# Sliding-window attention by key-value group, with both query blocks in one step

## The chip, the cores and the metric

The kernel runs on one core of a Trainium2 chip. The metric is the time of one execution on the device, in microseconds (us). The core has a matrix engine (PE in the profile, with its weight loads as PEld), three engines for elementwise work (DVE, ACT, POOL) and queues for transfers (DMA) between the device memory and the on-chip memory. PE writes into eight banks of accumulator memory; a bank holds 512 float32 values in each of 128 partitions, and DVE and ACT read the results from there. The granted PE clock of the profiled execution was 0.999 of full speed.

## The reference, cut to what matters

The program is one decoder layer over 256 tokens with 2048 features: a feed-forward block, a mixer (windowed attention beside a recurrent part), a look-up into a memory, a second feed-forward block and a norm. The change touches only the windowed attention inside the mixer. It has 16 query heads of 64 values, in four groups that share one key-value head each, and works in blocks of 128 queries, so there are two query blocks. A query sees at most the 128 latest positions, and each head has a learned "sink" that joins the softmax:

```python
s = jnp.einsum('bnqhgd,bnkhd->bnhgqk', qb, kb).astype(jnp.float32) * (HEAD_DIM ** -0.5)
valid = (dist >= 0) & (dist < WINDOW) & (blk * BLOCK + ki - BLOCK >= 0)
s = jnp.where(valid[None, :, None, None], s, NEG_INF)
m = jnp.maximum(jnp.max(s, axis=-1, keepdims=True), sink)
e = jnp.exp(s - m)
p = e / (jnp.sum(e, axis=-1, keepdims=True) + jnp.exp(sink - m))
o = jnp.einsum('bnhgqk,bnkhd->bnqhgd', p.astype(v.dtype), vb)
```

The first query block has 128 keys to look at, the second 256. The result, 256 tokens by 1024 values, goes into the product with `w_proj_attn`.

## The kernel before, in words

All large products go through `product` (line 420). It takes the weights two chunks of 128 rows at a time (an "item", line 401): a transfer brings the float32 chunk, ACT rounds it to a short part `hi` (line 365), DVE subtracts to get the rest `lo` (line 366), and `multiply` (line 446) issues six matmuls for each half of the tokens: `hi` by `hi` (line 442), `lo` by `hi` (line 443) and `hi` by `lo` (line 444), each 512 columns wide, or 288 in the product called "small". `AHEAD` is 2: `next_item` also writes the splitting of the next two items, and the split tiles have three buffers.

Everything else is written between those matmuls. `Interleave` (line 56) holds named groups of Python generators. After each call of `multiply` comes one `tick`, in which the first generators of each group, up to the group's limit, advance by one `yield`. The group "attn" has the limit 2, so two attention generators are under way at a time. A tick is thus six matmuls of a product and then a few steps of side work.

That is only the order of writing. The framework's planner then lays out each engine's list: at each point of its own reckoned time, an engine gets the instruction that was written first among those whose inputs and buffers the planner takes to be ready. On the chip each engine runs its list in order and waits where something is late. So side work written early can stand late in an engine's list, between the matmuls of a later tick.

The side work in question is `attend(kv, qb)` (line 940), called for four key-value groups `kv` and two query blocks `qb`, eight generators in all. Since two run at a time, the two query blocks of one group advance side by side, in the same ticks. One generator does this:

- **Scores**, line 949: the four query heads of a group are two chunks `c` by two halves `e` of the 128 partitions. Each matmul uses the 64 partitions of its half. The half `e=0` writes one bank and the half `e=1` another, both from the ring `mm`, which has three banks. The profile shows each of these float32 matmuls as two instructions.
- **Scale and mask**, line 955 (DVE), out of the banks into a tile `s`.
- **Softmax**: the maximum on DVE (line 962), small operations on four values per partition (lines 965 to 969), then the exponentials with their sums on ACT (lines 972 and 974), one for each head, and the division on DVE (lines 979 to 982).
- **Transposes**, line 988, of the probabilities through a bank of the ring `tr`, which has two banks, and a copy out on ACT (line 991).
- **Values**, line 996: 64 output partitions for each half `e`, into one `tr` bank, then a rounded copy on ACT (line 1003) and the rest on DVE (line 1004) into `ya`.

The ring `tr` also serves `feat` (line 623, the transposes at line 630) for other side work. The flag "attn", set when the last values are written, lets `decay_and_rate` (line 1055) begin, whose matmuls at line 1073 take banks from `mm`. The products under way meanwhile are "small" (288 columns, 16 ticks) and the two that make the recurrent keys (512 columns, 16 ticks each). `ya` is first needed four products later.

Of the kernel before, what the change touches and what calls it, by code (L numbers as in the profile page):

```python
# [15 lines left out]
P = 128  # L16
T = 256
# [119 lines left out]
def decoder_layer(ctx: ExitStack, tc: tile.TileContext, a: dict, out: bass.AP):  # L137
    nc = tc.nc
    act, dve, pool, pe = nc.scalar, nc.vector, nc.gpsimd, nc.tensor
# [17 lines left out]
    def f32(x):  # L157
        return x.bitcast(F32)
# [4 lines left out]
    def mm():  # L163
        return ps.tile([P, 512], F32, tag="mm", name="mm")

    def tr():
        return ps.tile([P, 512], F32, tag="tr", name="tr", bufs=2)

    def wait_for(name):
        while name not in bg.seen:  # L170
            yield

    def idle(n):
        for _ in range(n):
            yield
# [19 lines left out]
    ident = cpool.tile([P, P], F32, name="ident")  # L195
# [74 lines left out]
    for entry in weight_plan(a):  # L270
# [4 lines left out]
        w, k0, nk, c0, n = entry  # L275
# [16 lines left out]
    at = {"item": 0, "product": 0, "pool": None}  # L292
# [580 lines left out]
    with tc.tile_pool(name="mx", bufs=1, reuse_waits="tile") as sp:  # L873
# [3 lines left out]
        def t4(name, shape=(P, 4, T), dt=F32):  # L877
            return sp.tile(list(shape), dt, tag="t4", name=name, bufs=N4)
# [38 lines left out]
        qt = []  # L917
# [5 lines left out]
        kd = t4("kd")  # L923
        vt = t4("vt", (P, 2, KV_W))
# [12 lines left out]
        ya = act_tiles("ya", 2)  # L937
        sink4 = sinks[:].rearrange("p (k c e) -> p k e c", k=4, c=2)

        def attend(kv, qb):  # L940
            yield from wait_for("kv")
            w = P * (qb + 1)
            tq = slice(qb * P, qb * P + P)
            s = t4("s", (P, 2, 2, T))
            b = [mm() for _ in range(2)]
            for c in range(2):
                for e in range(2):
                    r = slice(64 * e, 64 * e + 64)
                    pe.matmul(  # L949
                        b[e][:, c * w : (c + 1) * w], qt[kv // 2][r, 2 * (kv % 2) + c, tq],  # L950
                        kd[r, kv, :w], start=True, stop=True,
                    )
            bias = abias[:, 1 - qb :, :].rearrange("p a b -> p (a b)")
            for e in range(2):
                dve.scalar_tensor_tensor(
                    s[:, e, :, :w], b[e][:, : 2 * w].rearrange("p (c w) -> p c w", c=2), 0.125,
                    bias.unsqueeze(1).to_broadcast([P, 2, w]), ALU.mult, ALU.add,
                )
            yield
            s3 = s[:].rearrange("p e c w -> p (e c) w")  # L960
            m = stat.tile([P, 4], F32, tag="m", name="m")
            dve.tensor_reduce(m[:], s3[:, :, :w], AX.X, ALU.max)
            sk = sink4[:, kv]
            m22 = m[:].rearrange("p (e c) -> p e c", e=2)
            dve.tensor_tensor(m22, m22, sk, ALU.max)
            nm = stat.tile([P, 4], F32, tag="nm", name="nm")
            dve.tensor_scalar(nm[:], m[:], -1.0, None, ALU.mult)
            es = stat.tile([P, 4], F32, tag="es", name="es")
            dve.tensor_tensor(es[:].rearrange("p (e c) -> p e c", e=2), sk, m22, ALU.subtract)
            yield  # L970
            den = stat.tile([P, 4], F32, tag="den", name="den")
            act.activation(es[:], es[:], AF.Exp)
            for i in range(4):
                at["exp"] = act.activation(
                    s3[:, i, :w], s3[:, i, :w], AF.Exp, bias=nm[:, i : i + 1],
                    accum_out=den[:, i : i + 1],
                )
            yield
            dve.tensor_tensor(den[:], den[:], es[:], ALU.add)
            dve.reciprocal(den[:], den[:])  # L980
            for i in range(4):
                dve.tensor_scalar(s3[:, i, :w], s3[:, i, :w], den[:, i : i + 1], None, ALU.mult)
            yield from idle(2)
            pt = t4("pt", (P, 2, 4, P))
            for kb in range(qb + 1):
                b = tr()
                for i in range(4):
                    pe.transpose(
                        b[:, i * P : (i + 1) * P], s3[:, i, kb * P : (kb + 1) * P], ident[:]
                    )  # L990
                act.copy(pt[:, kb], b[:].rearrange("p (i q) -> p i q", i=4))
            yield from idle(2)
            b = tr()
            for kb in range(qb + 1):
                for e in range(2):
                    pe.matmul(
                        b[64 * e : 64 * e + 64, : 2 * P], vt[:, kb, kv * 64 : kv * 64 + 64],
                        pt[:, kb, 2 * e : 2 * e + 2, :].rearrange("p c q -> p (c q)"),
                        start=kb == 0, stop=kb == qb,
                    )  # L1000
            b3 = b[:, : 2 * P].rearrange("p (c q) -> p c q", c=2)
            hi, lo = (ya.at(p, 2 * kv, 2)[:, :, tq] for p in range(2))
            act.copy(hi, b3)
            dve.tensor_tensor(lo, b3, f32(hi), ALU.subtract)
            if qb:
                ya.done |= {2 * kv, 2 * kv + 1}
            if kv == 3 and qb:
# [528 lines left out]
        for n in range(4):  # L1536
            g, m = t4("gl", (P, 2, 512)), t4("ml", (P, 2, 512))
# [21 lines left out]
        for n in range(4):  # L1559
            s = t4("x2", (P, 2, 512))  # L1560
# [16 lines left out]
        pt = [t4("ptm") for _ in range(2)]  # L1577
# [45 lines left out]
        for h in (0, 2):  # L1623
            b = tr()
# [17 lines left out]
    with tc.tile_pool(name="f2", bufs=1, reuse_waits="tile") as sp:  # L1642
# [51 lines left out]
        for t in range(2):  # L1694
            m, r = (stat.tile([P, 1], F32, tag=e, name=e) for e in ("ms", "rs"))
# [58 lines left out]
```

## Time and profile before

| | |
|---|---|
| median of three runs | 2233.55 us (2233.27 to 2233.9) |
| the profiled execution | 2234.97 us, of which 2233.2 us from the first to the last instruction |
| PE busy | 2218.3 us, 99% of the span |
| DVE busy | 1828.1 us, 82% |
| ACT busy | 1248.2 us, 56% |
| score matmuls, line 949 | 64 instructions, from 782.8 to 831.8 us |
| transposes, line 988 | 48 instructions, from 792.6 to 841.7 us |
| value matmuls, line 996 | 48 instructions, from 796.8 to 848.4 us |

All times within the profile count from its first instruction. In the lines of the timeline the first number is the start, the second the length, then come engine, line, operation, the tile written and the tiles read, the shape, and how many instructions of one kind in a row the line stands for. Matmuls overlap, so the length of one says little; the distance from one start to the next is the time that it takes of PE.

### The profile page before, as it was taken

The page shows a single profiled execution, that of the slowest core. Times are in us where ns is not written, and L with a number is a line of the kernel's source. Part 1 is how long each engine was busy: PE and PEld are TensorE (multiplying, and loading weights), DVE is VectorE, ACT ScalarE, POOL GpSimd, SP SyncE. Part 2 cuts the span into 40 slices and gives each one's busy share as a digit, 9 for nine tenths or more (in the row PEclk, how much of TensorE's full clock was granted, in tenths as well). Part 3 has the DMA queues.
Part 4 walks back from the last instruction along what each step waited for, and adds up shares of the span by engine and source line. Part 5 has one row for each costly group of instructions (what it writes and reads, how often), then busy time and mean ns, then how long its engine had stood idle before and what let it go on. Part 6 is the DMA issues. An engine that isn't in the chain of part 4 may idle for free.

```text
span 2233.2 us, 28140 instructions
## 1 busy us (share of the span) xinstructions
PE 2218.3 (99%) x10520; PEld 1825.6 (82%) x10520; DVE 1828.1 (82%) x2366; ACT 1248.2 (56%) x1626; POOL 116.6 (5%) x181
## 2 busy tenths in 40 slices
PE   9999999999999999999999999999999999999998
PEld 7888888888888877788888888888888888888876
DVE  7999989898989477877657656547999999999997
ACT  7555555555556468544444546556665565655654
POOL 0000000000001001200221030001000000000000
PEclk9999999999999999999999999999999999999999
DMA  8565566556556545677768688658575576556563
GB/s 303 193 211 199 189 208 201 194 189 212 202 189 199 173 134 153 188 236 208 225 202 277 200 262 282 188 160 279 195 251 194 193 245 207 203 208 220 198 240 137
DMA packets 231561, 466.02 MB, mean 209 GB/s; under 512 B 15521, under 2 KB 17921, under 8 KB 231425
## 3 DMA queue, kind: packets, MB, share of 16 engines
q1 hardware_dynamic: 222256, 438.08, 59.3%
q0 software_dynamic: 7648, 23.52, 3.4%
q10 hardware_dynamic: 1520, 2.63, 0.3%
q8 instruction: 82, 1.34, 0.3%
q14 instruction: 55, 0.44, 0.1%
HBM read 440.49 MB, written 23.59 MB: 208 GB/s over the span
## 4 chain that ended last, share of the span: by engine, by line
PE 91%; DVE 4%; DMA 3%; issue 1%; ACT 1%; SPq 0%; POOL 0%; POOLq 0%; ACTq 0%; DVEq 0%
PE acc L442 18%; PE acc L443 18%; PE acc L444 18%; PE mm L442 8%; PE mm L443 8%; PE mm L444 8%; PE tr L443 2%; PE tr L630 2%; PE tr L442 2%; PE tr L444 2%; DVE lo L366 2%; PE mm L1390 1%; DMA raw<-in_ffn_w_up_dram 1%; PE tr L1326 1%; PE mm L949 0%
## 5 line engine op out<-in xcount | busy, mean ns | idle before, releaser
L365 ACT CAST hi<-raw 128x1024 fp32r<-128x1024 f32 (+1 forms) x768 | 754.9, 993 | 685.6 <-PE acc L444 500.9
L366 DVE TENSOR_TENSOR lo<-raw,hi 128x1024 fp32r<-128x1024 f32 (+1 forms) x768 | 882.5, 1152 | 298.7 <-ACT hi L365 296.2
L442 PE MATMUL acc<-hi,xhi 128*128 128x512 f32 (+1 forms) x1134 | 446.9, 395 | 2.3 <-ACT hi L365 0.8
L443 PE MATMUL acc<-lo,xhi 128*128 128x512 f32 (+1 forms) x1134 | 440.5, 389 | 0.8 <-DVE lo L366 0.8
L444 PE MATMUL acc<-hi,xlo 128*128 128x512 f32 (+1 forms) x1134 | 440.2, 388 | 0.0
L442 PEld LDWEIGHTS acc<-hi,xhi 128*128 128x128 f32 x1134 | 212.8, 188 | 49.4 <-issue 3.7
L443 PEld LDWEIGHTS acc<-lo,xhi 128*128 128x128 f32 x1134 | 213.1, 188 | 44.9 <-DVE lo L366 2.1
L444 PEld LDWEIGHTS acc<-hi,xlo 128*128 128x128 f32 x1134 | 213.0, 188 | 44.2 <-issue 1.3
L373 ACT CAST thi<-raw 128x1024 fp32r<-128x1024 f32 x192 | 200.3, 1052 | 75.2 <-DVE raw L396 50.6
L374 DVE TENSOR_TENSOR tlo<-raw,thi 128x1024 fp32r<-128x1024 f32 x192 | 232.1, 1217 | 0.8 <-ACT thi L373 0.2
L442 PE MATMUL mm<-hi,xhi 128*128 128x512 f32 x402 | 156.6, 389 | 0.0
L443 PE MATMUL mm<-lo,xhi 128*128 128x512 f32 x402 | 156.5, 389 | 0.0
L444 PE MATMUL mm<-hi,xlo 128*128 128x512 f32 x402 | 156.4, 389 | 0.0
L444 PE MATMUL acc<-hi,hlo 128*128 128x512 f32 x372 | 145.4, 391 | 0.0
L443 PE MATMUL acc<-lo,hhi 128*128 128x512 f32 x372 | 145.3, 391 | 0.0
L442 PE MATMUL acc<-hi,hhi 128*128 128x512 f32 x372 | 145.0, 390 | 0.0
L442 PEld LDWEIGHTS mm<-hi,xhi 128*128 128x128 f32 x402 | 75.5, 188 | 16.3 <-ACT hi L365 0.5
L443 PEld LDWEIGHTS mm<-lo,xhi 128*128 128x128 f32 x402 | 75.5, 188 | 15.8
L444 PEld LDWEIGHTS mm<-hi,xlo 128*128 128x128 f32 x402 | 75.5, 188 | 15.7
L443 PEld LDWEIGHTS acc<-lo,hhi 128*128 128x128 f32 x372 | 69.8, 188 | 14.4
L444 PEld LDWEIGHTS acc<-hi,hlo 128*128 128x128 f32 x372 | 69.9, 188 | 14.1
L442 PEld LDWEIGHTS acc<-hi,hhi 128*128 128x128 f32 x372 | 69.9, 188 | 14.1
(400 smaller groups left out, 3548.7 us busy)
## 6 DMA issues: line engine op xcount, KB each, us to landing
raw<-in_ffn_w_down_dram SPq DMA_DIRECT2D x88, 1024.0 KB, 5.2
raw<-in_ffn_w_gate_dram SPq DMA_DIRECT2D x84, 1024.0 KB, 5.2
raw<-in_ffn_w_up_dram SPq DMA_DIRECT2D x78, 1024.0 KB, 6.1
raw<-in_w_in_dram SPq DMA_DIRECT2D x136, 512.0 KB, 3.7
raw<-in_w_out_dram SPq DMA_DIRECT2D x32, 512.0 KB, 4.8
raw<-sums SPq DMA_DIRECT2D x20, 512.0 KB, 6.3
raw<-in_w_proj_attn_dram SPq DMA_DIRECT2D x16, 512.0 KB, 4.3
raw<-in_w_proj_rwkv_dram SPq DMA_DIRECT2D x16, 512.0 KB, 6.0
```

The lines of the kernel that those rows point to most:

```text
L365: at["hi"] = act.copy(hi[:, s], raw[:, s])
L366: at["lo"] = dve.tensor_tensor(lo[:, s], raw[:, s], f32(hi[:, s]), ALU.subtract)
L373: act.copy(hi[:], v[:])
L374: dve.tensor_tensor(lo[:], v[:], f32(hi[:]), ALU.subtract)
L442: pe.matmul(o, xh, hi, start=first, stop=False, **how)
L443: pe.matmul(o, xh, lo, start=False, stop=False, **how)
L444: pe.matmul(o, xl, hi, start=False, stop=last, **how)
L630: pe.transpose(b[:, o : o + P], tok[:, t, col : col + P], ident[:])
L1326: pe.matmul(b[e][:, o : o + P], x1[r, j, cs_], x2[r, j, cs_], start=True, stop=True)
L1390: pe.matmul(vb[:, (o + k) * P : (o + k + 1) * P][:, r], lhs(k, e), rhs[:, k, r], start=first and k + e == 0, stop=True, **ek,)
```

## The change

`attend` now takes a key-value group alone and does both query blocks in one generator, so there are four generators, not eight. Odd groups first idle five ticks, so the two generators under way are at different steps.

- The scores of the first query block go into two banks of the ring `tr`, those of the second into two banks of `mm`, and all are written in one step.
- The small softmax operations work on both blocks at once (eight values per partition). The large ones (scale and mask, maximum, exponentials, division) stay one for each block or head, but stand in one step for both blocks. After the exponentials comes an idle tick more.
- The transposes of the first block and those of the second are written in two successive ticks.
- The values of both blocks go into one `tr` bank, with one copy and one subtraction of 512 columns in place of two of 256.

```diff
-        def attend(kv, qb):
+        def attend(kv):
             yield from wait_for("kv")
...
+            yield from idle(5 * (kv % 2))
+            s, b = [], []
+            for qb, bank in enumerate((tr, mm)):
+                w, tq = P * (qb + 1), slice(qb * P, qb * P + P)
+                s.append(t4("s", (P, 2, 2, T)))
+                b.append([bank() for _ in range(2)])
+                for c in range(2):
+                    for e in range(2):
+                        r = slice(64 * e, 64 * e + 64)
+                        pe.matmul(
+                            b[qb][e][:, c * w : (c + 1) * w], qt[kv // 2][r, 2 * (kv % 2) + c, tq],
+                            kd[r, kv, :w], start=True, stop=True,
+                        )
+            for qb in range(2):
...
+                for e in range(2):
+                    dve.scalar_tensor_tensor(
+                        s[qb][:, e, :, :w], b[qb][e][:, : 2 * w].rearrange("p (c w) -> p c w", c=2),
+                        0.125, bias.unsqueeze(1).to_broadcast([P, 2, w]), ALU.mult, ALU.add,
+                    )
+            yield
...
+            for qb in range(2):
+                dve.tensor_reduce(m[:, qb], s3[qb], AX.X, ALU.max)
...
+            yield
             act.activation(es[:], es[:], AF.Exp)
+            for qb in range(2):
+                for i in range(4):
+                    at["exp"] = act.activation(
+                        s3[qb][:, i], s3[qb][:, i], AF.Exp, bias=nm[:, qb, i : i + 1],
+                        accum_out=den[:, qb, i : i + 1],
+                    )
+            yield from idle(2)
             dve.tensor_tensor(den[:], den[:], es[:], ALU.add)
             dve.reciprocal(den[:], den[:])
+            for qb in range(2):
+                for i in range(4):
+                    dve.tensor_scalar(
+                        s3[qb][:, i], s3[qb][:, i], den[:, qb, i : i + 1], None, ALU.mult
+                    )
             yield from idle(2)
+            pt = []
+            for qb in range(2):
+                pt.append(t4("pt", (P, 2, 4, P)))
+                for kb in range(qb + 1):
+                    t_ = tr()
...
+                    act.copy(pt[qb][:, kb], t_[:].rearrange("p (i q) -> p i q", i=4))
+                yield
+            yield
+            o = tr()
+            for qb in range(2):
+                for kb in range(qb + 1):
+                    for e in range(2):
+                        pe.matmul(
+                            o[64 * e : 64 * e + 64, 2 * qb * P : 2 * (qb + 1) * P],
+                            vt[:, kb, kv * 64 : kv * 64 + 64],
+                            pt[qb][:, kb, 2 * e : 2 * e + 2, :].rearrange("p c q -> p (c q)"),
+                            start=kb == 0, stop=kb == qb,
+                        )
...
+            act.copy(hi, o4)
+            dve.tensor_tensor(lo, o4, f32(hi), ALU.subtract)
...
         for kv in range(4):
-            for qb in range(2):
-                bg.spawn("attn", attend(kv, qb))
+            bg.spawn("attn", attend(kv))
```

More of the change, by code (lines that the diff above doesn't have):

```diff
@@ new lines, in attend @@
+            yield
+            s3 = [
+                s[qb][:].rearrange("p e c w -> p (e c) w")[:, :, : P * (qb + 1)] for qb in range(2)
+            ]
+            m, nm, es, den = (
+                stat.tile([P, 2, 4], F32, tag=name, name=name) for name in ("m", "nm", "es", "den")
+            )
+            for qb in range(2):
+                dve.tensor_reduce(m[:, qb], s3[qb], AX.X, ALU.max)
+            sk = sink4[:, kv].unsqueeze(1).to_broadcast([P, 2, 2, 2])
+            m4 = m[:].rearrange("p b (e c) -> p b e c", e=2)
@@ L983, in attend @@
-            yield from idle(2)
[L984 to L1007, printed above, removed]
+            for qb in range(2):
[3 more added lines that the diff above has]
+                    )
@@ new lines, in attend @@
+            yield from idle(2)
+            pt = []
[3 more added lines that the diff above has]
+                    t_ = tr()
+                    for i in range(4):
+                        pe.transpose(
+                            t_[:, i * P : (i + 1) * P], s3[qb][:, i, kb * P : (kb + 1) * P],
+                            ident[:],
+                        )
+                    act.copy(pt[qb][:, kb], t_[:].rearrange("p (i q) -> p i q", i=4))
+                yield
@@ L1008, in attend @@
+            o4 = o[:].rearrange("p (b c q) -> p c b q", b=2, c=2)
+            hi, lo = (
+                ya.at(p, 2 * kv, 2).rearrange("p c (b q) -> p c b q", b=2) for p in range(2)
+            )
+            act.copy(hi, o4)
+            dve.tensor_tensor(lo, o4, f32(hi), ALU.subtract)
+            ya.done |= {2 * kv, 2 * kv + 1}
+            if kv == 3:
                 bg.seen.add("attn")
         for kv in range(4):
-            for qb in range(2):
-                bg.spawn("attn", attend(kv, qb))
+            bg.spawn("attn", attend(kv))
```

38 lines of the change are left out of this document (5 added, 33 removed).

## The prediction

> **What bounds the kernel now.** I read the page first, for the engine that is the limit and for the chain of work that ended last.
>
> ```profile
> span 2233.2 us, 28140 instructions
> ...
> PE 2218.3 (99%) x10520; PEld 1825.6 (82%) x10520; DVE 1828.1 (82%) x2366; ACT 1248.2 (56%) x1626; POOL 116.6 (5%) x181
> ...
> PE 91%; DVE 4%; DMA 3%; issue 1%; ACT 1%; SPq 0%; POOL 0%; POOLq 0%; ACTq 0%; DVEq 0%
> ```
>
> PE is busy for 99% of the span, and the chain is PE for 91%. So the change is worth what it takes from PE's own list, plus or minus the waits that it puts there or removes. What it saves on DVE and ACT is worth nothing by itself. Next I grouped the score matmuls by shape, between 780 and 852 us; this is the row of the wide ones, and there are as many narrow ones.
>
> ```profile
> L949 PE MATMUL mm<-kd,qt 64*128 64x256 f32 x32 | 8.9, 399 | 0.0
> ```
>
> Each of the four groups of heads has 8 instructions of 128 columns (first query block) and 8 of 256 (second). The change removes none of them, nor any transpose or value matmul. It can only change how they stand to each other, so I then went through PE's timeline, where the start of one line to the start of the next is what it costs. The first group:
>
> ```profile
> 782.47 0.29 PE L443 MATMUL acc<-lo,xhi 128*128 128x288 f32 x1
> 782.60 0.29 PE L444 MATMUL acc<-hi,xlo 128*128 128x288 f32 x1
> 782.82 1.57 PE L949 MATMUL mm<-kd,qt 64*128 64x128 f32 x12
> 784.33 0.40 PE L442 MATMUL acc<-hi,xhi 128*128 128x288 f32 x1
> 784.57 0.29 PE L443 MATMUL acc<-lo,xhi 128*128 128x288 f32 x1
> 784.79 1.13 PE L949 MATMUL mm<-kd,qt 64*128 64x256 f32 x4
> 785.85 0.40 PE L444 MATMUL acc<-hi,xlo 128*128 128x288 f32 x1
> ```
>
> The ring `mm` has three banks and the two generators want four. So twelve instructions go at 782.82, and the four of the last bank come at 784.79, when DVE has emptied a bank. Those four take 785.85 − 784.79 = 1.06 us, 0.265 us each. The fourth group shows what two halves cost when they do stand side by side:
>
> ```profile
> 825.83 0.72 PE L949 MATMUL mm<-kd,qt 64*128 64x128 f32 x8
> 826.78 1.20 PE L988 MATMUL tr<-ident,s 128*128 128x128 f32 x8 [0.24 <-DVE s L982]
> 827.91 1.13 PE L949 MATMUL mm<-kd,qt 64*128 64x256 f32 x4
> 828.97 1.52 PE L996 MATMUL tr<-pt,vt 128*64 128x256 f32 x12
> 830.41 0.50 PE L442 MATMUL acc<-hi,xhi 128*128 128x512 f32 x1
> ...
> 831.08 1.13 PE L949 MATMUL mm<-kd,qt 64*128 64x256 f32 x4
> 832.13 0.50 PE L444 MATMUL acc<-hi,xlo 128*128 128x512 f32 x1
> ```
>
> The values at 828.97 are also 256 columns wide and use the two halves of the array in turn: 12 of them take 830.41 − 828.97 = 1.44 us, 0.12 each, against 0.265 for scores of the same width that have only one half. Matmuls on two halves run together; alone, each pays in full. The second query block never has both its banks at once, in any group (see below, too). That is where PE time lies.
>
> **The change part by part.**
>
> *Scores in one group of sixteen.* With four banks free, the 128-column instructions of both halves and the 256-column ones of both halves stand side by side. The first group's twelve hold the eight narrow ones in pairs and four wide ones of one half alone; the four wide ones of the other half would run beside those at no further cost, as the values do. So I take 784.33 − 782.82 = 1.51 us for the whole sixteen. The groups two and three now:
>
> ```profile
> 792.17 0.49 PE L949 MATMUL mm<-kd,qt 64*128 64x128 f32 x4
> 792.60 0.55 PE L988 MATMUL tr<-ident,s 128*128 128x128 f32 x3
> 793.07 0.48 PE L949 MATMUL mm<-kd,qt 64*128 64x128 f32 x2
> 793.49 0.33 PE L988 MATMUL tr<-ident,s 128*128 128x128 f32 x1
> 793.75 1.14 PE L949 MATMUL mm<-kd,qt 64*128 64x128 f32 x6
> 794.81 0.40 PE L442 MATMUL acc<-hi,xhi 128*128 128x288 f32 x1
> ...
> 799.03 1.13 PE L949 MATMUL mm<-kd,qt 64*128 64x256 f32 x4
> 800.09 0.41 PE L444 MATMUL acc<-hi,xlo 128*128 128x288 f32 x1
> ```
>
> ```profile
> 803.85 0.71 PE L949 MATMUL mm<-kd,qt 64*128 64x128 f32 x6
> 804.49 0.50 PE L443 MATMUL acc<-lo,xhi 128*128 128x512 f32 x1
> ...
> 805.84 1.13 PE L949 MATMUL mm<-kd,qt 64*128 64x128 f32 x6
> 806.91 0.50 PE L442 MATMUL acc<-hi,xhi 128*128 128x512 f32 x1
> ...
> 815.89 1.13 PE L949 MATMUL mm<-kd,qt 64*128 64x256 f32 x4
> 816.95 0.50 PE L442 MATMUL acc<-hi,xhi 128*128 128x512 f32 x1
> ```
>
> Group one: 1.51 + 1.06 = 2.57. Group two: 794.81 − 792.17 = 2.64, less four transposes at (827.91 − 826.78)/8 = 0.14, is 2.07, and 1.06 more: 3.13. Group three: 0.64 + 1.07 + 1.06 = 2.77. Group four: 826.78 − 825.83 less the 0.24 of waiting is 0.71, then 1.06 and 1.05: 2.82. In all 11.3 us. After: 4 × 1.51 = 6.0. **Gain 5.3 us.** The bounds: 0, if the four banks are never free together, and 5.3, since the first group's twelve are the best that the trace has.
>
> *Visits.* Each time PE goes from the product to this work and back it loses a little. Going in: 782.82 − 782.60 = 0.22 in place of 0.13; coming out: 784.57 − 784.33 = 0.24 in place of 0.13. That is 0.20 us a visit. The scores now take nine visits (2, 2, 3, 2 in the four groups) and then four, which saves 5 × 0.20 = 1.0. But two of the nine are shared with transposes or values, which would then need a visit of their own: 0.4 back. **Gain 0.6 us.** The bounds: 1.0, and −0.6 if the transposes, now written in two ticks, split into five more visits than I count. The Trainium skill, "TensorEngine Tiling (Array Packing)", section "Key Properties" under "Tiling Modes", says that a change of tiling mode empties the array; the 0.20 us agrees in kind. From the roughly 166 ns of fixed latency that "TensorE: Matmul & The Clock Gate" of the Trainium skill gives under "Single matmul latency", two changes a visit would be an estimated 0.33 us; the visits would then give 1.0 and the sum would be 0.4 lower.
>
> *Small operations, copies and values.* Five kinds of small DVE operation and one of ACT now run 8 times and will run 4 times.
>
> ```profile
> L967 DVE TENSOR_SCALAR nm<-m 128x4 f32<-128x4 f32 x8 | 1.3, 160 | 0.0
> ```
>
> At about 0.16 us each that is 20 × 0.16 = 3.2 us of DVE, and the eight copies become four wider ones. PE covers it all, so the price is nothing; if PE's cover were gone, it would be a gain. The values stand twelve in a row already (828.97), so one bank instead of two gives PE nothing. No transfer is added or moved, and POOL and SP have no part in it.
>
> *Waits.* The division for all eight heads now stands behind the last of the eight exponentials, where before the first block's began when four were done. The place to look is the first group, where the product "small" is narrow (a tick is 6 × 0.13 = 0.8 us). Of ACT's timeline, of DVE's, and of the waits between 783 and 849 us:
>
> ```profile
> 789.47 0.40 ACT L974 ACTIVATE s<-s,nm 128x128 f32<-128x128 f32 x1
> ...
> 793.18 0.66 ACT L365 CAST hi<-raw 128x576 fp32r<-128x576 f32 x1
> ```
>
> ```profile
> 791.66 0.87 DVE L982 TENSOR_SCALAR s<-s,den 128x128 f32<-128x128 f32 x4
> ...
> 794.77 2.09 DVE L366 TENSOR_TENSOR lo<-raw,hi 128x576 fp32r<-128x576 f32 x3
> ```
>
> ```profile
> DVE den L979 <- ACT s L974: 5.7, 6, 2.1
> ```
>
> ACT is taken by exponentials from 789.47 to 793.18, 3.7 us, and rounds no weights meanwhile; DVE gets to the next `lo` at 794.77. From 792.17 to 794.81 PE lives on scores and transposes alone (the rows of group two): it had run out of split weights and had 2.6 us of side work to cover that, without idling. After the change the four divisions of 791.66 (0.87 us) also come after 793.18, so the `lo` comes about 0.8 later, near 795.6. From 792.2 that is 3.4 us to cover, and there is one block of scores, 1.51, and some 0.6 of transposes. **A loss of 1.3 us**, bounded by 0 (covered, as now) and 3.4 here. Queued behind the waiting division on DVE are the `lo` of the next items, and PE's product waits for those. Further on the products are 512 wide and an item lasts twice as long, so I count it once.
>
> *The sum:* −5.3 − 0.6 + 1.3 = −4.6 us. The profiled execution has a span of 2233.2 and 1.8 around it, 2234.97 in all, which is 1.4 above the median of the runs; the difference is taken off the median: 2233.55 − 4.6 = **2229.0 us**, a span of about 2228.6.
>
> **The rivals.**
>
> *The ring `tr` is short.* The first block's scores now need both banks of `tr`, which transposes, values and `feat` also use, and the groups overlap. If one is taken, the narrow scores go one half at a time, as at 803.85 and 805.84, in visits of their own: 0.64 + 0.20 and more, about 1.0 us a group. With two or three of the later groups so, 2 to 3 us of the gain are gone: **2231.0 to 2232.0**. For it: the idle five ticks put one group's scores right before the transposes of the other. Against: a scale-and-mask operation empties a bank within about half a microsecond, and in the first group nothing else wants them. The Trainium skill, same tiling page, "Gotcha 1: PSUM Pressure" under "Restrictions and Gotchas", speaks for this rival: row tiles must write different banks, so tiling raises the need for them. By that rule it would hold in every group with an overlap; the trace has such a case, the fourth bank of 784.79.
>
> *Starved PE, slower than before.* By the 16 ticks of "small" the change has begun three groups, where it had been two: groups start at ticks 0, 5, 10 and 20 in place of 0, 8, 16 and 24. Each brings 3.7 us of exponentials, in which ACT rounds nothing; the lead of two items is worth only 2 × 1.6 = 3.2 us there. If three groups each left PE uncovered for 3.7, that is 11.1, and against the 5.9 gained the kernel would be 5.2 slower: **2238.8**. It decides from 5.9 us of waiting on. Against: the stretch has room,
>
> ```profile
> 782.80:803.50 20.70, 20.70 (x141) 17.14 (x141) 15.51 (x39) 12.78 (x32) 0.00 (x0) 1.00 0.43 131
> ```
>
> DVE is busy for 15.5 of 20.7 us and ACT for 12.8. And a wait of one group's leaves another's scores and transposes to do.
>
> *Nothing gained.* The pairs form, but the side work comes in a worse order later: PE's one long wait of the stage, for the tokens of "small",
>
> ```profile
> PE tr L630 <- ACT tok L892: 0.8, 1, 0.8
> ```
>
> shows that a list laid out ahead can be wrong by that much. Four or five such would eat the gain: **2233.5**.
>
> **How the numbers follow.** Forecast (all or nearly all sixteen together, one to two microseconds of waiting): 0.52, from 2227.0 to 2230.5, likeliest 2229.0. Short ring: 0.20. Nothing gained: 0.16. Starved: 0.12. The bound of 0.2%, about what a measurement here can tell from no change, is 4.5 us: 2229.1. The forecast straddles it, with the greater part below if the waits stay small; I give 0.44 to faster, all of it from the forecast, 0.08 + 0.20 + 0.16 = 0.44 to same, 0.12 to slower. The range goes from 2226.5 (both gains at their best, 6.3, and 0.8 more if the wait for the tokens goes too) to 2235.0, which takes in the short ring and nothing gained. The forecast's own range is 2227.0 to 2230.5.
>
> **What would show it.** Right: four lines of sixteen score instructions, each about 1.5 us to the next line. PE at line 949 from 11.3 to about 6 us. An idle stretch of about a microsecond on PE near 794, ended by `lo` of line 366. Wrong: score lines of 4 or 8, waits of PE for `lo` in more than one group, or the score lines whole and the span unchanged, which would send me to the later side work.

## The result, and the profile after

The changed kernel takes 2237.18 us in the median of 22 runs (2235.25 to 2243.43), and the kernel before beside it 2234.51 us (2233.27 to 2235.28, 22 runs). The ratio is 1.0014, with a 95% interval from 1.0008 to 1.0021: slower by 3.1 us by the ratio and by 2.7 us between the medians, within the 0.2% that I called no change and gave a chance of 0.44. The forecast of 2229.0 was 8.2 us too low and the range, up to 2235.0, missed the time by 2.2 us. The profiled execution of the changed kernel is the longest of its 22, 2243.43 us, 6.3 us above the median; so its profile shows more loss than most of its runs have. The page:

```profile
span 2241.7 us, 28113 instructions
...
PE 2220.8 (99%) x10520; PEld 1828.0 (82%) x10520; DVE 1827.8 (82%) x2342; ACT 1247.4 (56%) x1618; POOL 117.4 (5%) x181
...
PE 91%; DVE 4%; DMA 2%; ACT 1%; issue 1%; POOL 0%; SPq 0%; POOLq 0%; DVEq 0%; ACTq 0%
```

The page looks like the one before. PE is busy 2.5 us longer for the same 10520 instructions, and the span less PE's busy time went from 14.9 to 20.9 us. A page cannot say where. For that I set the matmuls of the large products into `acc` side by side: there are 5862 in both kernels and in the same order, so the start of the nth in one against the nth in the other is a clock that the side work cannot blur.

| start before (us) | start after less start before (us) |
|---|---|
| 784.3 | −0.03 |
| 863.5 | −4.27 |
| 957.1 | −5.48 |
| 1099.5 | −5.50 |
| 1168.5 | +1.85 |
| 1238.5 | +8.43 |
| 1300.7 | +6.68 |
| 1812 | +7.02 |
| 2215 | +8.55 |

There are two stories. By 957 us the change has earned 5.5 us. It keeps them until 1099.5, and between there and 1300 the kernel loses 12.2 us, in a stage that the diff doesn't touch. Another 1.9 us goes in small steps after that, 1.2 of it between 2058 and 2123.

*The attention stage.* PE's timeline after, at the first three groups (start, length, engine, line, operation, tiles, shape; in brackets PE's idle time and what ended it):

```profile
782.60 0.79 PE L951 MATMUL tr<-kd,qt 64*128 64x128 f32 x7
...
783.34 1.03 PE L951 MATMUL mm<-kd,qt 64*128 64x256 f32 x7
784.29 0.40 PE L442 MATMUL acc<-hi,xhi 128*128 128x288 f32 x1
...
788.48 0.72 PE L951 MATMUL tr<-kd,qt 64*128 64x128 f32 x8
789.03 1.03 PE L951 MATMUL mm<-kd,qt 64*128 64x256 f32 x8
789.99 0.40 PE L442 MATMUL acc<-hi,xhi 128*128 128x288 f32 x1
...
794.43 0.30 PE L1000 MATMUL tr<-ident,s 128*128 128x128 f32 x1 [0.97 <-DVE s L990]
...
796.84 0.70 PE L951 MATMUL mm<-kd,qt 64*128 64x256 f32 x4
797.47 1.51 PE L1011 MATMUL tr<-pt,vt 128*64 128x256 f32 x12
798.91 0.60 PE L951 MATMUL tr<-kd,qt 64*128 64x128 f32 x3
...
799.99 0.40 PE L442 MATMUL acc<-hi,xhi 128*128 128x288 f32 x1
...
801.55 0.71 PE L951 MATMUL tr<-kd,qt 64*128 64x128 f32 x4
```

Groups one and two stand sixteen together and take 1.69 and 1.51 us to the next product matmul. The third is split: four wide instructions alone at 796.84, eight behind the values of another group, four narrow ones alone at 801.55. The fourth group, sixteen in a row again, goes at 819.43 and takes 2.12 us. PE idles for 0.97 us at 794.43.

*The later stage.* PE's waits after, from 780 to 1400 us (in total, times, longest):

```profile
PE tr L630 <- ACT tok L892: 3.2, 1, 3.2
PE acc L443 <- DVE lo L366: 2.2, 2, 1.6
PE tr L1000 <- DVE s L990: 1.0, 1, 1.0
```

The third is the idle of the attention. The two others are at 1121 and 1183 us, in the recurrence (the second row has 0.6 us from another place). PE's timeline there:

```profile
1117.62 0.39 PE L444 MATMUL acc<-hi,xlo 128*128 128x512 f32 x1
1121.25 0.44 PE L630 MATMUL tr<-ident,tok 128*128 128x128 f32 x2 [3.25 <-ACT tok L892]
```

```profile
1180.96 0.39 PE L442 MATMUL acc<-hi,xhi 128*128 128x512 f32 x1
1182.98 0.50 PE L443 MATMUL acc<-lo,xhi 128*128 128x512 f32 x1 [1.64 <-DVE lo L366]
```

A wait of 3.25 and one of 1.64 make 4.9 of the 12.2 us. The rest shows in the stretches of 20 us, with the granted clock third from the end; first the kernel before, then the one after:

```profile
1120.00:1140.00 20.00, 20.00 (x171) 18.05 (x169) 11.47 (x19) 7.89 (x14) 1.46 (x3) 1.00 0.69 225
1180.00:1200.00 20.00, 20.00 (x128) 16.96 (x129) 17.05 (x24) 11.23 (x18) 2.56 (x5) 1.00 0.96 339
```

```profile
1120.00:1140.00 20.00, 18.67 (x146) 17.12 (x147) 8.25 (x14) 9.31 (x17) 4.55 (x7) 0.91 0.47 157
1180.00:1200.00 20.00, 18.26 (x98) 15.64 (x98) 14.15 (x17) 7.95 (x13) 3.33 (x6) 0.83 0.75 275
```

After each of the two waits the clock is lower for some microseconds: 20 × 0.09 = 1.8 us and 20 × 0.17 = 3.4 us lost. Idle time from 1080 to 1260 (5.7 us after, 0.4 before) and clock (5.2) make 10.5 of the 12.2 us. The other 1.7 I have not put to a line.

*What the two waits wait for.* The first, in ACT's waits, SP's timeline and the list of transfers (size, median time from issue to landing) of the kernel after, and then the same copy in the kernel before (times of one in ns: shortest, median, longest; first and last start):

```profile
ACT tok L892 <- DMA sums<-sg: 4.9, 1, 4.9
```

```profile
1113.64 0.46 SPq L358 DMA_DIRECT2D sums<-sg  x1
```

```profile
sums<-sg SPq DMA_DIRECT2D x1, 512.0 KB, 6.8
```

```profile
L892 ACT ACTIVATE tok<-acc,rs x2: 688/691/694, 1111.0 to 1113.1; 128x512 f32<-128x512 f32 x2
```

This is the staging (`stage`, line 337): it loads a pair of weight tiles `su` and `sg` for a later product, lets DVE form sums and differences of them (lines 350 to 355), and writes them out (line 358). Its tiles come from the same ring `t4` as the token copy `tok`, and the copy got the buffer that the write-out had still to read: issued at 1113.64, landed 6.8 us later, and the copy starts at 1120.5. (SP issues in the order of its list, and here a load of other weights, which went at 1113.22 when DVE had freed its buffer, stands ahead of the write-out.) Before, the copy starts at 1111.0 without a transfer to wait for.

The second, in DVE's and SP's timeline after, with the time from issue to landing of the load at 1168.58:

```profile
1176.18 0.42 DVE L1500 TENSOR_TENSOR gl<-g,gh 128x256 fp32r<-128x256 f32 x1
1179.90 0.69 DVE L350 TENSOR_TENSOR sg<-su,sg 128x512 f32<-128x512 f32 x1 [3.30 <-issue]
...
1181.71 1.22 DVE L366 TENSOR_TENSOR lo<-raw,hi 128x1024 fp32r<-128x1024 f32 x1
```

```profile
1168.58 0.45 SPq L346 DMA_DIRECT2D sg<-in_ffn_w_gate_dram  x1
...
1173.38 0.42 SPq L346 DMA_DIRECT2D su<-in_ffn_w_up_dram  x1
...
1174.90 0.56 SPq L346 DMA_DIRECT2D sg<-in_ffn_w_gate_dram  x1
```

```profile
sg<-in_ffn_w_gate_dram SPq DMA_DIRECT2D x1, 512.0 KB, 11.2
```

There are ten pairs, loaded and subtracted in order, and this is the fifth. Its loads were issued at 1168.05 and 1168.58; the second landed 11.2 us later, at 1179.82, and the subtraction starts at 1179.90. The four loads from 1173.38 to 1174.90 are those of the next two pairs, issued while this one was still under way. DVE has the subtraction in its list ahead of that landing: it stands for 3.3 us with the `lo` of the next weights behind it, and PE waits for that `lo`. In the kernel before, the loads of this pair were issued at 1148.80 and 1149.36 and had landed by 1154.9, long before DVE came to the subtraction at 1169.60.

Why does an edit in the attention reach this? The flag "attn" comes with the last values. By the steps of the generators the last group now ends at tick 29 of the side work, where it ended at 31, so `decay_and_rate` and all that follows it (recurrent keys, their inverse, the token copies) begin two ticks earlier, while the staging is written from fixed items on (`STAGE_AT`, line 42). The two share the ring `t4`, DVE's list and the DMA queues, and stand differently to each other. That was the theory; the experiments test it.

### The profile page after: what moved, and what is told of

It reads as the page before. It is cut to its first block, busy times and chain, and to the rows that moved or that the text cites. A ratio compares the mean times of both kernels' runs of the same rounds, so it can differ in the third digit from the quotient of the medians.

```text
span 2241.7 us, 28113 instructions
## 1 busy us (share of the span) xinstructions
PE 2220.8 (99%) x10520; PEld 1828.0 (82%) x10520; DVE 1827.8 (82%) x2342; ACT 1247.4 (56%) x1618; POOL 117.4 (5%) x181
## 4 chain that ended last, share of the span: by engine, by line
PE 91%; DVE 4%; DMA 2%; ACT 1%; issue 1%; POOL 0%; SPq 0%; POOLq 0%; DVEq 0%; ACTq 0%
PE acc L442 18%; PE acc L443 18%; PE acc L444 18%; PE mm L443 8%; PE mm L442 8%; PE mm L444 8%; PE tr L443 2%; PE tr L630 2%; PE tr L442 2%; PE tr L444 2%; DVE lo L366 2%; PE mm L1406 1%; DMA raw<-in_ffn_w_up_dram 1%; PE tr L1342 1%; ACT hi L365 1%
```

## The experiments

All were run in five rounds beside the kernel before, which had medians from 2234.19 to 2234.60 us in them.

**The flag two ticks later, in the kernel after.**

```diff
+                yield from idle(2)
                 bg.seen.add("attn")
```

> The changed kernel, with two idle ticks before the flag "attn" is set, so that the chain of side work behind it (decays, keys, inverse, recurrence) begins in the same tick as before the change. Theory A (the attention gains its 5.3 us, and the two ticks by which the chain now starts earlier cost more than that, because a token copy then waits for the transfers of the staging work and PE goes idle): the gain stays and the loss goes, about 2228.5 us, 8 to 9 us under the changed kernel; the copy at line 892 near 1118 us waits for no transfer, no PE wait over 1 us between 1080 and 1260. Theory B (the loss comes from the attention's own new tiles, its bunched ACT and DVE work or its use of the shared buffers): the loss stays, 2236 to 2238 us.

2232.53 us (2230.32 to 2233.93), ratio 0.999 (0.9981 to 0.9999). The two waits are gone, the clock is 1.00 in both stretches, and nothing is lost between 1080 and 1260. The time is still 4 us above the 2228.5 of theory A; 2.2 us of the early gain are missing in its profile. Half of them went by 862, with a new wait near 841; from PE's waits, 780 to 1080:

```profile
PE tr L630 <- ACT tok L892: 1.8, 1, 1.8
```

Ahead of it ACT waits 2.3 us for a transfer at line 1149. The other half is missing between 862 and 957, where the changed kernel gains 1.2 us and this one nothing. So the place of the flag decides over the late loss, and it decides over other gains and waits as well.

**The flag two ticks earlier, in the kernel before.** It is set after the last transposes, not after the last values; the attention stays as it was.

```diff
+            if kv == 3 and qb:
+                bg.seen.add("attn")
...
-            if kv == 3 and qb:
-                bg.seen.add("attn")
```

> The kernel before, with the flag "attn" set two ticks earlier (after the last transposes are written and not after the last values); the attention itself is as before. Theory A: this alone brings the loss, 8 us more than the kernel before, 2240 to 2244 us, with the token copy at line 892 waiting for a staging transfer and PE idle for about 3 us there. Theory B: within 2 us of the kernel before.

2243.78 us (2240.72 to 2249.44, five runs, of which the profile shows the longest), ratio 1.004 (1.0026 to 1.0053). Between 1075 and 1280 it loses 9.3 us, in the same two places; the waits from 1080 to 1260 show it:

```profile
DVE sg L350 <- issue: 3.5, 1, 3.5
ACT tok L892 <- DMA sums<-sg: 3.2, 1, 3.2
PE acc L443 <- DVE lo L366: 1.9, 1, 1.9
```

It loses another 7.0 us at 840 to 862, where the changed kernel gains, so its total isn't a measure of the change. But the late loss comes without a line of the new attention, and so do the 1.2 us gained between 862 and 957.

The transfers say the same. Taken against the product matmuls beside them, on the clock of the kernel before, the loads of the staging's fifth pair come at 1148.8 us in the kernel before and in the changed kernel with the flag late, and at 1164.9 us in the changed kernel and in the kernel before with the flag early. The flag sets their place, whichever attention runs.

**Four banks alone, in the kernel before.** The first query block's banks come from `tr`; all else stays.

```diff
-            b = [mm() for _ in range(2)]
+            b = [(mm if qb else tr)() for _ in range(2)]
```

> The kernel before, with one edit: the scores of the first query block take their two banks from the ring tr, those of the second from mm. Eight generators, ticks and flag as before. Theory A: the four banks are the whole gain, so the scores stand in lines of sixteen and the time is 2228 to 2230 us, 4 to 5.5 under the kernel before. Theory B, or if the merged steps are needed for the gain: scores broken into lines of 4 and 8 still, 2231 to 2234 us.

2239.09 us (2238.16 to 2240.14), ratio 1.002 (1.0012 to 1.0029): slower than either theory had it. The first group stands sixteen together and takes 1.68 us, against the 1.51 of the prediction. The later groups stand in sixes, twos and fours, since `tr` also serves transposes and values, and PE waits twice for the tokens of "small" (780 to 1080):

```profile
PE tr L630 <- ACT tok L892: 2.6, 2, 1.5
```

The kernel is 5.2 us behind by 866 us and loses nothing later. So the rival of the short ring is real when the four banks come without the other steps.

**The staging one item earlier, in the kernel after.**

```diff
-STAGE_AT = [266 + 2 * n for n in range(10)]
+STAGE_AT = [265 + 2 * n for n in range(10)]
```

> The changed kernel, with the staging work (loads, subtractions and write-outs of the sums for the second feed-forward block) begun one item, which is two ticks, earlier, so that staging and chain stand to each other as before, but both two ticks earlier against the products. Theory A in its strict form (it is the meeting of staging and chain that costs): the loss goes, 2228 to 2231 us. If what matters is where the staging transfers stand to the token copy, a part of the product sequence, the copy still waits for one of them and some 3 to 8 us of loss stay: 2232 to 2237 us. Theory B: 2236 to 2238 us.

**2229.20 us** (2228.45 to 2229.75), ratio 0.9975 (0.9966 to 0.9985): faster than both kernels. The offset of −5.5 us at 957 is there again from 1280 to the end (−5.3 to −5.7), the clock is 1.00 in all stretches from 1080 to 1260, and what is left of the copy's wait (1080 to 1260) is

```profile
ACT tok L892 <- DMA sums<-sg: 0.4, 1, 0.4
```

The attention and the flag are untouched, so the loss lies in how the staging stands to the work around it.

**The same in the kernel before**, to see whether an earlier staging is simply faster.

> The control for e4: the kernel before, with nothing changed but the staging work begun one item earlier. Theory A (what costs is the meeting of the earlier chain with the staging transfers; staging has no cost of its own in the kernel before): within 1.5 us of the kernel before, 2233 to 2236 us, and no PE wait over 1 us between 1080 and 1260. Rival C (the staging begun earlier is itself what made e4 fast, whatever the attention): 2228 to 2230 us.

2242.73 us (2239.48 to 2245.82), ratio 1.0037 (1.0025 to 1.0049). It isn't, nor is it without effect, as theory A had it; in the kernel before the same edit makes the loss, 9.8 us after 1075, with DVE again in front of the subtraction and PE behind it at the masked matmuls:

```profile
PE tr L1363 <- DVE mk L1332: 4.3, 2, 3.2
DVE sg L350 <- issue: 3.3, 1, 3.3
```

**The staging one item later (267), in the kernel after.**

> The changed kernel, with the staging work begun one item later. Here, as the list is laid out, the token copy at line 892 near 1118 us takes a buffer that no transfer holds. Theory A in the form that the copy's buffer decides: no wait at that copy, 2229 to 2232 us. Theory A in its strict form (chain and staging must stand to each other as before): now four ticks apart, the loss stays or grows, 2236 us or more.

2229.31 us (2228.82 to 2232.41), ratio 0.998 (0.9971 to 0.9989). Earlier or later by one item makes no difference; of 265, 266 and 267, 266 is the bad place for this attention. The strict form of theory A, that staging and chain must stand to each other as before, fails here.

**Two items later (268), in the kernel after, and two earlier (264), in the kernel before.** They were to tell a plain rule of phase (an item is two ticks, and the pairs come every four) from a rule about the token copy.

> The changed kernel, with the staging work begun two items (four ticks) later. Theory P (the staging brings a new pair every four ticks, and what decides is where in those four ticks the chain stands; fast so far at distances of 0 and 4 ticks from that of the kernel before, slow at 2 either way): the distance is 6, the middle of the four again, so PE waits come back between 1080 and 1260 and the time is 2234 to 2243 us. Rival T (what decides is the token copy near 1118 us and the buffer that it gets): the copy gets a buffer that no transfer holds, as in e6, so 2228.5 to 2231 us.

> The kernel before, with the staging work begun two items (four ticks) earlier. Theory P: the distance is 4 ticks, so it is as fast as the kernel before, 2232.5 to 2236 us, where one item earlier (e5) cost 8.5. Rival T: the token copy takes a buffer that a staging write-out holds, as in the changed kernel, so PE waits for it and the kernel is slower by 3 us or more, 2237 to 2243 us.

2234.16 us (2232.16 to 2238.73), ratio 0.9999 (0.999 to 1.0008), and 2239.05 us (2238.08 to 2240.68), ratio 1.0021 (1.0013 to 1.003). The waits from 1080 to 1260, first at 268 after, then at 264 before:

```profile
DVE sg L350 <- issue: 3.6, 1, 3.6
PE acc L443 <- DVE lo L366: 2.0, 1, 2.0
```

```profile
DVE sg L350 <- DMA sg<-in_ffn_w_gate_dram: 3.2, 1, 3.2
PE tr L1363 <- DVE mk L1332: 2.8, 1, 2.8
```

Neither rule holds in both. The phase rule wanted 264 to be fast in the kernel before, and it isn't; the rule about the copy wanted 268 to be fast, and a wait at the copy in 264, and neither came. What the slow kernels (the changed one, the flag early, 265 and 264 before, 268 after) have in common is that DVE stands at line 350 for more than three microseconds; in the kernel before, and at 265 and 267 after, no such wait of DVE's is there. In each of the five the subtraction starts within 0.2 us of the landing of its second tile, whose load took 9.3 to 11.6 us.

**The write-out two ticks earlier, in the kernel after.**

```diff
             dve.tensor_tensor(g1, g1, u1, ALU.subtract)
-        yield from idle(8)
+        yield from idle(6)
```

> The changed kernel; in the staging work alone the write-out of a finished pair of sums comes one item (two ticks) earlier, loads and subtractions stay. Theory A: the transfer that the token copy waits for is over about one item, 2.7 us of product and more with the side work, sooner, so the wait of 3.2 us there falls under 0.6 us, and the clock stays up there. The second wait, for lo near 1183, hangs on the staging loads and may stay, with its clock loss: 2231 to 2236 us. If the wait at the copy is not the cause, 2236 to 2238 us.

2235.21 us (2233.39 to 2237.31), ratio 1.0004 (0.9996 to 1.0013). Both waits are still there (1080 to 1260), only shorter:

```profile
PE tr L630 <- ACT tok L892: 2.1, 1, 2.1
PE acc L443 <- DVE lo L366: 1.3, 1, 1.3
```

The wait for the copy was to fall under 0.6 and fell by 1.1 only.

**The subtraction two ticks later, in the kernel after.** Loads and write-outs keep their ticks.

```diff
-        yield from idle(4)
+        yield from idle(6)
         u0, u1, g0, g1 = (e[:, c] for e in t for c in range(KU))
...
-        yield from idle(8)
+        yield from idle(6)
```

> After, with the staging's subtraction two ticks later (the stage item idles 6 ticks before its subtraction, not 4, and 6 after it, not 8, so that loads and write-outs keep their ticks). Theory L (VectorE's list has the subtraction L350 ahead of the landing of its transfer; the lo of the next weight tile stands behind it, TensorE waits for lo and then runs at a lower granted clock): the 3.3 us wait at L350 near 1176 to 1180 and TensorE's 1.6 us wait for lo near 1183 go, the granted clock of 1180 to 1200 is 0.98 or more, and the time is 2232 to 2235 us; the 3.2 us wait for the token copy near 1121 stays, because its write-out is issued at the same tick. Theory Q (the loads themselves and the traffic beside them hold TensorE back, the place of the subtraction does not matter): the wait moves to another instruction, and the time stays at 2236 to 2238 us.

2234.35 us (2231.64 to 2235.51), ratio 0.9998 (0.9989 to 1.0008): 2.8 us less than the changed kernel. DVE now has the `lo` that stood behind the subtraction ahead of it, and runs the subtraction without a wait:

```profile
1174.29 1.22 DVE L366 TENSOR_TENSOR lo<-raw,hi 128x1024 fp32r<-128x1024 f32 x1
...
1177.01 0.68 DVE L350 TENSOR_TENSOR sg<-su,sg 128x512 f32<-128x512 f32 x1
```

PE has no wait for `lo` from 1100 to 1260, and the clock from 1180 to 1200 is 1.00. Theory L is borne out, but the edit moved the traffic too: the pair's loads are issued at nearly the same place, yet the second lands after 8.3 us in place of 11.2, at 1174.96, and the loads of the next two pairs go only from 1176.02 on. That DVE doesn't wait here, both can explain. That PE doesn't wait needs no more than the new place in DVE's list, since its `lo` no longer stands behind the subtraction; no run moved the place alone.

**The same, with the write-out four ticks earlier.**

```diff
-        yield from idle(8)
+        yield from idle(2)
```

> After, with the staging's subtraction two ticks later and its write-out four ticks earlier; the loads, the attention and the flag stay where they are. Theory A (the two waits near 1121 and 1183, with the lower granted clock behind each, are all that the staging costs): the wait of TensorE for the token copy falls below 1.2 us, the wait for lo stays away, the granted clock of 1120 to 1140 and of 1180 to 1200 is 0.97 or more, and the time is 2229 to 2232 us, near the kernel with the staging one item earlier (2229.2). Rival R (something else between 1080 and 1260 is lost that moving the loads or the flag cures, and these waits do not): the time stays at 2233 to 2235 us, as with the later subtraction alone (2234.35).

2234.80 us (2232.56 to 2235.79), ratio 1.0001 (0.9992 to 1.001). This experiment doesn't decide, because its edit didn't do what it was for: the write-out follows the subtraction, which is later for the first pair too, so it was issued only at 1115.2 and the copy's wait stayed at 2.2 us.

**The first pair apart**: its subtraction stays and its write-out comes six ticks earlier; for all other pairs the subtraction is two ticks later.

```diff
-        yield from idle(4)
+        yield from idle(4 if n == 0 else 6)
...
-        yield from idle(8)
+        yield from idle(2 if n == 0 else 6)
```

> After, with the staging's subtraction two ticks later for all pairs but the first, and the first pair's write-out six ticks earlier (its subtraction stays, so that the write-out can follow it at once). Loads, attention and flag stay. Theory A (the two waits near 1121 and 1183 and the lower granted clock behind them are all that is lost): TensorE's wait for the token copy is below 0.8 us, the wait for lo stays away, and the time is 2229 to 2232 us, as with the staging one item earlier (2229.2). Rival R (something else between 1080 and 1260 is lost, which moving the staging or the flag cures and these waits do not): the waits are gone as well, and the time stays at 2233 to 2235 us.

2232.36 us (2231.74 to 2234.05), ratio 0.999 (0.9981 to 0.9999): 4.8 us less than the changed kernel, but 3.2 more than with the staging one item earlier. The condition was again missed, and this time the profile says why; from PE's waits and from the transfers near it:

```profile
PE tr L630 <- ACT tok L892: 2.0, 1, 2.0
```

```profile
sums<-sg SPq DMA_DIRECT2D x1, 512.0 KB, 8.4
```

The write-out is issued at 1110.96, 2.7 us earlier than in the changed kernel, and takes 8.4 us in place of 6.8: it lands 1.0 earlier. The loads of the second pair, 512 KB each, were issued right ahead of it, at 1109.62 and 1110.14. That the write-out shares the transfer engines with them is the likely reason; a run with those loads moved alone wasn't made. So the copy's wait hangs on the staging's traffic, and no write-out tick tried here removes it; moving the staging does. By the medians the late loss is 2237.18 − 2229.20 = 8.0 us. In this kernel, without the wait for `lo`, 4.8 of them are back. For the other 3.2 there is a wait of 2.0 us for the copy, which the kernel with the staging at 265 doesn't have; the last 1.2 us I can't place, so it stays open whether the two waits are the whole.

This kernel and the one with the subtraction later alone have almost the same waits (2.0 and 2.2 us for the copy, none for `lo`), and still 2.0 us between their medians. Their mean clocks differ: 0.999 in 10 of 11 runs here, 0.998 in 7 of 11 there. The last section comes back to that.

**No stagger.** The kernel with the staging at 265, without the idle five ticks of the odd groups; ten idle ticks before the flag keep the flag near its place.

```diff
-            yield from idle(5 * (kv % 2))
...
+                yield from idle(10)
                 bg.seen.add("attn")
```

> The kernel of e4 without the five idle ticks of the odd groups; ten idle ticks before the flag keep the start of the chain where it is in e4. Two groups then go through the same steps in the same ticks and want the two banks of tr and four of mm at once. Theory D (four banks alone do not pay, as e3 showed; the stagger is what lets the ring tr serve them): scores and transposes break into pieces again, PE waits come back, 2232 to 2238 us. If the merged steps are enough: within 1.5 us of e4.

2235.04 us (2233.76 to 2236.67), ratio 1.0004 (0.9995 to 1.0012): 5.8 us more than with it. PE's waits, 780 to 1080:

```profile
PE acc L443 <- DVE lo L366: 2.2, 2, 1.7
PE tr L999 <- DVE s L989: 1.9, 1, 1.9
```

With two groups in step, PE waits for the division and for split weights in the attention: the rival of the starved PE, which the stagger keeps away.

## Why the prediction was wrong

Within the stage that I priced, it came out close. Taking each PE instruction from its start to the next one's, and adding by line between the same two product matmuls (782.6 to 957.1 before, 782.4 to 951.7 after):

- *Scores in one group of sixteen*, forecast 5.3: line 949's 11.35 us became 7.69, a gain of 3.7. Groups one and two took 1.69 and 1.51, where 1.51 was forecast. The third is the rival of the short ring, in one group, for which I had given 1.0 a group; the fourth took 2.12.
- *Visits*, forecast 0.6, and *Waits*, forecast −1.3: product matmuls together with the idle ahead of them cost 0.2 us less. The idle stretch near 794 was there, 0.97 us. The division ended it, not `lo`: PE was waiting at the transposes that stand ahead of the product in its list. The 0.8 us for the tokens of "small" went, so the waits came out even, where I had seen a loss.
- Not in the sum: the transposes cost 0.5 us less (4.93 to 4.42) and the matmuls of the recurrent keys 1.0 less (line 1195, now 1211: 5.57 to 4.60). The latter come with the earlier flag and not with the new attention: the kernel before with the flag early has 4.60 there too, the changed kernel with the flag late 5.56.
- *The sum*: 5.3 us on PE against 4.6. With the staging moved by one item and nothing else, the kernel measured 2229.20 and 2229.31 us; the forecast was 2229.0. That they meet is in part luck: the scores gave 1.6 us less than forecast, and the waits that came out even and the terms that were not in the sum made up for it.

The step that failed is in *Small operations, copies and values*: "No transfer is added or moved, and POOL and SP have no part in it". None is added, but they are moved, and I had put that at nothing. The flag at the end of the attention came two ticks earlier, and with it everything that waits for the flag; around that work the staging's transfers and its subtractions in DVE's list came to other places. The loads of the fifth pair went from 1148.80 to 1168.05 us, and the next two pairs' from 1170.19 and 1182.81 to 1173.38 and 1174.36, right behind them. I had named the flag in describing the kernel and had no term for it. Its price in the profiled execution is 12.2 us, and by the medians 8.0 (2237.18 − 2229.20).

The rival *nothing gained* had the right kind, side work in a worse order later, and the wrong size: it took the 0.8 us wait for one set of tokens as the price of a bad place. Here one bad place cost 3.25 us, and one 1.64 us, and the lower clock behind both cost as much again. *Starved PE* had the right sign for the wrong reason; it showed only without the stagger. What I had written to look for was of use: "the score lines whole and the span unchanged, which would send me to the later side work" is where it went.

## What to carry to other kernels

When an edit makes a stage end earlier, follow the flag that it sets, and price what starts there against everything with a fixed start that shares its buffers, its queues or its engine lists, not only the stage itself. A subtraction placed in an engine's list ahead of its transfer's landing holds all that is behind it; compare in the profile when its tiles land and what stands in line. A change that gains in its own stage and loses in another isn't finished: here the start of the staging, moved by one item either way, turned 2.7 us lost into 5 us gained.

## What the runs showed of the hardware

The granted clock fell after short waits, and not always. In the changed kernel the five microseconds behind the 1.64 us wait ran at half clock (stretch, length, busy times of PE, weight loads, DVE, ACT, POOL, clock, DMA share, GB/s):

```profile
1185.00:1190.00 5.00, 5.00 (x18) 4.42 (x18) 1.02 (x2) 0.96 (x2) 0.00 (x0) 0.50 1.03 391
```

and its product matmuls start 0.42 to 0.43 us apart there (1188.40, 1188.83, 1189.25) in place of 0.23. But behind almost equal waits for the token copy, 2.16 us with the subtraction later and 2.23 us with the write-out earlier too, the clock was once 0.91 and once 1.00; first the one, then the other:

```profile
1120.00:1140.00 20.00, 19.92 (x152) 18.17 (x153) 8.52 (x14) 8.95 (x17) 4.55 (x7) 0.91 0.43 146
```

```profile
1120.00:1140.00 20.00, 19.92 (x167) 18.02 (x165) 8.75 (x15) 9.62 (x18) 4.55 (x7) 1.00 0.50 171
```

So the same wait costs 1.8 us more (20 × 0.09) in one execution than in another. That fits the spread of the kernels with waits: the changed one goes from 2235.25 to 2243.43 over its runs with mean clocks from 0.999 down to 0.996, and the one with the staging at 265 only from 2228.45 to 2229.75, all at 0.999. The Trainium skill, "TensorE: Matmul & The Clock Gate", "Why this matters for your kernels", advises "No PE-idle gaps >~3µs between matmul bursts"; the 3.25 us wait agrees with it, the 1.64 us wait with half the clock behind it does not, and here the measurement decides. The same page says under "What's actually happening" that the window in which activity is judged runs free of the kernel; the unequal clock behind equal waits agrees with that, though no run here shows the window.
